# A hybrid attention and RG-LRU layer: the end of each recurrent block moved into the next block's projection

## The chip, the cores and the metric

The kernel runs on one core of one Trainium2 chip. The metric is the device time of one execution in microseconds (us). A TensorE clock of 1.00 in the profile is 2.4 GHz, 0.50 is 1.2 GHz.

## The reference, cut to what matters

One layer of a decoder on 16 meta tokens and 1024 tokens of width 2048. The normalised input goes through one projection to q, k, v, g_a, u and g_r; eight heads of differential attention and eight recurrent blocks of 128 channels are gated, put side by side and multiplied with `w_out`. The recurrent part is the one that the change touches:

```python
u = conv4(u) + conv_b                                  # causal, per channel
ub = u.reshape(B, T, N_LRU_BLOCKS, LRU_BLOCK)
r = sigmoid(einsum('btnc,ncd->btnd', ub, w_a) + b_a)   # two gates, a 128 x 128
i = sigmoid(einsum('btnc,ncd->btnd', ub, w_x) + b_x)   # matrix per block each
log_a = -LRU_C * r * softplus(-lru_lambda)
a = exp(log_a)
b = sqrt(-expm1(2.0 * log_a)) * i * u                  # factor 1 at position 0
h = scan(h = a * h + b)                                # over the positions
rec = h * silu(g_lru)
```

## The kernel before

Channels lie on the partitions, positions along the free dimension. The work is done in two halves: half A has the 16 meta tokens and 512 positions, half B the other 512. The order in time is: attention heads of A, recurrent blocks of A (some 463 to 642 us), attention heads of B, recurrent blocks of B (some 1111 to 1308 us, at first between the parts of the last head), then the output projection. Every matmul in fp32 is made of three in fp32r: the operands are split in a high and a low part (`split`, line 77: the high part by ScalarE, the low one by VectorE), and high x high, high x low and low x high are summed in PSUM.

`proj` (line 135) is one projection of 128 channels: 16 steps `kt` of three matmuls (L158 to L160), into one PSUM bank per job. `load_w` loads the weights in two parts of eight `kt` each: a raw tile by SyncE's queue (two buffers), then `whi` and `wlo` by `split` (three buffers each). A job names its bank by a tag: "proj" (two banks), "S" (three), "T" (two) or "pv" (one). `midway` is a function that `proj` calls after half of the steps; what it issues, and the matmuls behind it are tied to come after the instruction that it returns. Before the change only the first head used it.

A recurrent block is made by `lru` (line 523) of two projections, u and g. In half A u has two jobs, of 272 and 256 columns, one after the other; in half B it has one of 512. g has 512 columns in both. When the last job of u is done, its sink calls `finish` (line 464): the convolution in four steps on VectorE (L467, then L470 three times), the split into `uh` and `ul`, for each of the two gates three matmuls into banks "S" or "T" (L485 to L487; in half A twice, by columns) and a sigmoid (L488), and the recurrence up to the scan (L492 to L502). The sink of g (`g_sink`, line 509) takes `gx` from the bank (L512), and makes the sigmoid, the products and the DMA of the result (`emit_mix`, L430, on POOL's queue) that later work loads. The convolution's input `ue`, `uc`, `sg` and `gx` have one buffer each.

In half A two loads of half B's input (`step`, lines 175 to 191, scaled on ScalarE and VectorE in L187 to L190) and one for its squares (`squares`, L200) are issued on POOL's queue after each u projection, and tied to come after the last `emit_mix`. In half B loads of earlier results for the output projection (`load_mix`, L619) are issued after u and g of blocks 1 to 4, behind the last weight load on SyncE's queue.

Tiles and waits are set by a framework that also orders each engine's instructions at build time, by simulated times and buffers (`schedule_with_timeline_sim`, line 939); `issue_after` adds only an order on one engine's queue. So the order of the code isn't the order in the trace. In the last attention head of half B, `pv` collects the products with v (L405 to L407), `att` is read from it (L413), and `ms` takes the same single bank for the norm (L418, L419; read last by L424).

Of the kernel before, what the change touches and what calls it, by code (L numbers as in the profile page):

```python
# [66 lines left out]
class Trunk:  # L67
# [67 lines left out]
    def proj(self, *groups, midway=None):  # L135


        nc = self.nc
        work = []
        for m, jobs in groups:  # L140
            ws = self.load_in(m, 0, 2) if isinstance(m, int) else m
            if len(groups) == 1:
                work += [[(ws, j)] for j in jobs]
            else:
                work.append([(ws, j) for j in jobs])
        if len(groups) > 1:
            work = [sum(work, [])]
        for unit in work:
            acc = [self.ps.tile([P, 512], F32, tag=j[3], name="proj", bufs={"S": 3, "pv": 1}.get(j[3], 2)) for _, j in unit]
            with ExitStack() as order:  # L150
                for kt in range(KT):
                    if kt == 8 and midway:
                        order.enter_context(self.tc.issue_after(midway().ins))
                    c = slice((kt % 8) * P, (kt % 8) * P + P)
                    for (ws, (hT, c0, n, _, _)), ps in zip(unit, acc):
                        hi, lo = ws[kt // 8]
                        xh, xl = hT[0][kt][:, c0:c0 + n], hT[1][kt][:, c0:c0 + n]
                        nc.tensor.matmul(ps[:, :n], lhsT=hi[:, c], rhs=xh, start=(kt == 0), stop=False)  # L158
                        nc.tensor.matmul(ps[:, :n], lhsT=hi[:, c], rhs=xl, start=False, stop=False)  # L159
                        nc.tensor.matmul(ps[:, :n], lhsT=lo[:, c], rhs=xh, start=False, stop=(kt == KT - 1))  # L160
            for (_, j), ps in zip(unit, acc):
                j[4](ps)
# [279 lines left out]
    def lru_part(self, b, half, pool, tl, gw, carry):  # L442
# [7 lines left out]
        def u_sink(c0, w):  # L450
            def f(ps):
                if c0 == 0:
                    state["ue"] = ue = pool.tile([P, 3 + LA], F32, tag="ue", name="ue", bufs=1)
                    if half:
                        nc.vector.tensor_copy(out=ue[:, 0:3], in_=carry[:, 0:3])
                    else:
                        nc.vector.memset(ue[:, 0:3], 0.0)
                nc.vector.tensor_tensor(out=state["ue"][:, 3 + c0:3 + c0 + w], in0=ps[:, :w],
                                        in1=self.rstd[:, half * LA + c0:half * LA + c0 + w], op=ALU.mult)
                if c0 + w == n:  # L460
                    state["h"] = finish()
            return f

        def finish():
            ue = state["ue"]
            uc = pool.tile([P, LA], F32, tag="uc", name="uc", bufs=1)[:, :n]
            nc.vector.tensor_scalar(out=uc, in0=ue[:, 3:3 + n], scalar1=par[:, 3:4], scalar2=par[:, 4:5],  # L467
                                    op0=ALU.mult, op1=ALU.add)
            for i in range(3):
                nc.vector.scalar_tensor_tensor(out=uc, in0=ue[:, i:i + n], scalar=par[:, i:i + 1], in1=uc,  # L470
                                               op0=ALU.mult, op1=ALU.add)
            uh = tl.tile([P, n], F32R, tag="pth", name="uh", bufs=1 + half)
            ul = tl.tile([P, n], F32R, tag="ptl", name="ul", bufs=1 + half)
            self.split(uh, ul, uc)
            if not half:
                nc.vector.tensor_copy(out=carry[:, 0:3], in_=ue[:, n:n + 3])
            gates = []
            for g in range(2):
                o = tl.tile([P, n], F32, tag=("eg", "gr")[g], name="gate", bufs=gb)
                for c0, w in ([(0, 512)] if half else [(0, 272), (272, 256)]):  # L480
                    x = "T" if g and not half else "S"
                    ps = self.ps.tile([P, 512], F32, tag=x, name=x, bufs={"S": 3, "T": 2}[x])
                    c = slice(c0, c0 + w)
                    wh, wl = gw[0][:, g * P:(g + 1) * P], gw[1][:, g * P:(g + 1) * P]
                    nc.tensor.matmul(ps[:, :w], lhsT=wh, rhs=uh[:, c], start=True, stop=False)  # L485
                    nc.tensor.matmul(ps[:, :w], lhsT=wh, rhs=ul[:, c], start=False, stop=False)
                    nc.tensor.matmul(ps[:, :w], lhsT=wl, rhs=uh[:, c], start=False, stop=True)  # L487
                    nc.scalar.activation(o[:, c], ps[:, :w], AF.Sigmoid, bias=par[:, 5 + g:6 + g])  # L488
                gates.append(o)
            r, gi = gates  # L490
            th = tl.tile([P, n], F32, tag="tmp", name="th", bufs=gb)
            nc.scalar.activation(th, r, AF.Tanh, scale=self.negc[:, b:b + 1])  # L492
            nc.scalar.activation(r, r, AF.Exp, scale=self.posc[:, b:b + 1])
            d = pool.tile([P, LA], F32, tag="dd", name="dd", bufs=1 + half)[:, :n]
            nc.scalar.activation(d, r, AF.Square)
            nc.vector.scalar_tensor_tensor(out=th, in0=d, scalar=1.0, in1=th, op0=ALU.add, op1=ALU.mult)
            self.last_sqrt = nc.scalar.activation(th, th, AF.Sqrt)
            if not half:
                nc.vector.memset(th[:, 0:1], 1.0)
            nc.vector.tensor_tensor(out=gi, in0=gi, in1=uc, op=ALU.mult)  # L500
            nc.vector.tensor_tensor(out=gi, in0=gi, in1=th, op=ALU.mult)
            nc.vector.tensor_tensor_scan(out=d, data0=r, data1=gi,  # L502
                                         initial=carry[:, 3:4] if half else 0.0,
                                         op0=ALU.mult, op1=ALU.add)
            if not half:
                nc.vector.tensor_copy(out=carry[:, 3:4], in_=d[:, n - 1:n])
            return d

        def g_sink(ps):
            sg = pool.tile([P, HALF], F32, tag="sg", name="sg", bufs=1)  # L510
            gx = pool.tile([P, HALF], F32, tag="gx", name="gx", bufs=1)
            nc.vector.tensor_tensor(out=gx, in0=ps, in1=self.rstd[:, META + half * HALF:META + (half + 1) * HALF],  # L512
                                    op=ALU.mult)
            self.last_sigmoid = nc.scalar.activation(sg, gx, AF.Sigmoid)
            nc.vector.tensor_tensor(out=sg, in0=gx, in1=sg, op=ALU.mult)
            hst = state["h"]
            o = 0 if half else META
            nc.vector.tensor_tensor(out=sg, in0=sg, in1=hst[:, o:o + HALF], op=ALU.mult)
            self.emit_mix(half, H + b, sg)

        return u_sink, g_sink

    def lru(self, b, half, pool, tl, hT, tag="proj", g_tag="proj"):
        gw = self.lru_weights(b, pool)
        if not half:
            if b == 0:
                self.carry_all = self.const.tile([P, 32], F32, name="carry")
            self.carry[b] = self.carry_all[:, 4 * b:4 * b + 4]
        us, gs = self.lru_part(b, half, pool, tl, gw, self.carry[b])
        chunks = [(0, HALF)] if half else [(0, 272), (272, 256)]  # L530
        return ((M_U + b, [(hT, c0, w, tag, us(c0, w)) for c0, w in chunks]),
                (M_GR + b, [(hT, 0 if half else META, HALF, g_tag, gs)]))


    def setup0(self):
# [245 lines left out]
    def build(self):  # L781
# [67 lines left out]
        with ExitStack() as s:  # L849
            pool = s.enter_context(tc.tile_pool(name="lruA", bufs=1, side="left", reuse_waits="tile"))  # L850
            pb = s.enter_context(tc.tile_pool(name="prepB", bufs=1, side="left", reuse_waits="tile"))
            self.sq_bufs = 1
            step, squares, fin_b = self.prep(pb, nc.gpsimd, self.xb, HALF, 1, hTB, LA, 2)
            for b in range(8):
                for m, jobs in self.lru(b, 0, pool, pool, hTA):
                    self.proj((m, jobs))
                    if m < M_GR:
                        with tc.issue_after(self.last_mix.ins):
                            for i in range(2 * b, 2 * b + 2):
                                step(i)  # L860
                            squares(b)
            fin_b()
        left.close()

# [9 lines left out]
        m1 = fin.enter_context(tc.tile_pool(name="m1", bufs=1, side="left", reuse_waits="tile"))  # L874
        mixA = []
        with tc.tile_pool(name="lruB", bufs=1, side="left", reuse_waits="tile") as pool:
            for b in range(8):
                for m, jobs in self.lru(b, 1, pool, tl, hTB, *("T" if b == 1 else "proj",) * 2):
                    self.proj((m, jobs))
                    if 1 <= b < 5:  # L880
                        with tc.issue_after(self.last_w.ins):
                            for _ in range(2):
                                mixA.append(self.load_mix(m1, 0, len(mixA)))
        tail.close()
        right.close()
        ps_cm.__exit__(None, None, None)
# [56 lines left out]
```

## Time and profile before

| | us |
|---|---|
| median of three runs | 1642.99 |
| lowest and highest | 1640.56 and 1643.88 |
| the profiled execution | 1637.0 |
| its span, first to last instruction | 1635.2 |
| TensorE busy | 1596.9 |
| VectorE busy | 1117.6 |
| ScalarE busy | 874.1 |

Times in the rows are in us from the first instruction of the profiled execution. PE is TensorE, DVE VectorE, ACT ScalarE, POOL GpSimd, PEld TensorE's loading of weights. "[2.16 <-ACT uh L79]" at the end of a row means that the engine stood idle for 2.16 us before it, until ScalarE had written `uh` in line 79.

### The profile page before, as it was taken

What the parts mean: (1) busy time and instruction counts of PE and PEld (TensorE: products, weight loads), DVE (VectorE), ACT (ScalarE), POOL (GpSimd) and SP (SyncE); (2) the same over time, 40 slices, a digit from 0 to 9 for tenths busy, and PEclk for the clock granted to TensorE, in tenths of its full rate; (3) what the DMA queues carried; (4) which work ended last, traced back from release to release, by engine and by line L of the source; (5) the groups of instructions that cost most, each with busy time, mean ns of one, the idle gap of its engine ahead of it and who ended that gap; (6) DMA issues with size and microseconds to landing.
All of it is one profiled execution on the core that took longest, in us unless ns stands there. A gap on an engine that the chain in (4) does not pass through costs nothing.

```text
span 1635.2 us, 22985 instructions
## 1 busy us (share of the span) xinstructions
PE 1596.9 (98%) x8466; PEld 1370.8 (84%) x8466; DVE 1117.6 (68%) x2218; ACT 874.1 (53%) x1392; POOL 205.2 (13%) x308
## 2 busy tenths in 40 slices
PE   7999999999999999999999999999999999899996
PEld 6889889998989888888888888887887887788885
DVE  6766556665676667667668667757877656867996
ACT  5655555545566657456556556545776543332533
POOL 1211111110011010201011001000000002200262
PEclk9999999999999999999999999999999999999999
DMA  9633344333344443533234234233443388969874
GB/s 310 206 121 109 116 137 132 122 124 108 122 146 145 145 142 123 183 114 116 84 120 134 78 120 123 78 97 100 138 138 114 120 309 290 326 234 330 307 283 154
DMA packets 85196, 261.61 MB, mean 160 GB/s; under 512 B 11659, under 2 KB 13748, under 8 KB 84956
## 3 DMA queue, kind: packets, MB, share of 16 engines
q1 hardware_dynamic: 60544, 192.18, 35.2%
q0 software_dynamic: 24304, 67.90, 12.6%
q8 instruction: 67, 1.10, 0.3%
q14 instruction: 45, 0.37, 0.1%
q10 hardware_dynamic: 236, 0.06, 0.0%
HBM read 213.35 MB, written 39.86 MB: 155 GB/s over the span
## 4 chain that ended last, share of the span: by engine, by line
PE 75%; DVE 8%; issue 7%; DMA 7%; ACT 3%; POOL 1%; SPq 0%; ACTq 0%; DVEq 0%; POOLq 0%
PE proj L158 20%; PE proj L159 19%; PE proj L160 19%; PE T L396 2%; PE o L685 2%; PE o L686 2%; PE o L684 2%; DVE wlo L80 2%; PE S L341 2%; PE S L339 2%; DMA wb<-w_out 1%; DVE y L700 1%; DVE wb L658 1%; DMA xb<-mix_d 1%; DMA xt<-x 1%
## 5 line engine op out<-in xcount | busy, mean ns | idle before, releaser
L158 PE MATMUL proj<-hTA,whi 128*128 128x256 f32 (+2 forms) x1152 | 373.5, 325 | 1.9 <-ACT whi L79 1.9
L159 PE MATMUL proj<-hTA,whi 128*128 128x256 f32 (+2 forms) x1152 | 370.4, 322 | 0.0
L160 PE MATMUL proj<-hTA,wlo 128*128 128x256 f32 (+2 forms) x1152 | 369.5, 322 | 0.5 <-DVE wlo L80 0.5
L79 ACT ACTIVATE whi<-wraw 128x1024 fp32r<-128x1024 f32 (+1 forms) x218 | 228.2, 1047 | 244.8 <-PE proj L159 186.6
L80 DVE TENSOR_TENSOR wlo<-wraw,whi 128x1024 fp32r<-128x1024 f32 (+1 forms) x218 | 264.0, 1212 | 116.5 <-ACT whi L79 116.3
L158 PE MATMUL proj<-hTB,whi 128*128 128x512 f32 x768 | 302.1, 393 | 1.2 <-DVE gr L291 0.6
L160 PE MATMUL proj<-hTB,wlo 128*128 128x512 f32 x768 | 300.9, 392 | 0.0
L159 PE MATMUL proj<-hTB,whi 128*128 128x512 f32 x768 | 299.8, 390 | 0.0
L158 PEld LDWEIGHTS proj<-hTA,whi 128*128 128x128 f32 x1152 | 218.8, 190 | 18.7 <-ACT whi L79 2.6
L160 PEld LDWEIGHTS proj<-hTA,wlo 128*128 128x128 f32 x1152 | 218.7, 190 | 16.3 <-DVE wlo L80 0.7
L159 PEld LDWEIGHTS proj<-hTA,whi 128*128 128x128 f32 x1152 | 219.0, 190 | 14.4
L685 PE MATMUL o<-wlo,mix 128*128 128x512 f32 x416 | 163.2, 392 | 7.9 <-DVE wlo L80 7.9
L158 PEld LDWEIGHTS proj<-hTB,whi 128*128 128x128 f32 x768 | 144.3, 188 | 30.4 <-DVE gr L291 2.6
L160 PEld LDWEIGHTS proj<-hTB,wlo 128*128 128x128 f32 x768 | 144.2, 188 | 30.1
L159 PEld LDWEIGHTS proj<-hTB,whi 128*128 128x128 f32 x768 | 144.3, 188 | 28.6
L686 PE MATMUL o<-whi,mix 128*128 128x512 f32 x416 | 162.6, 391 | 0.0
L684 PE MATMUL o<-whi,mix 128*128 128x512 f32 x416 | 162.5, 391 | 0.0
L358 ACT ACTIVATE s<-s,st 128x144 f32<-128x144 f32 (+7 forms) x128 | 100.0, 782 | 50.9 <-DVE st L356 50.1
L685 PEld LDWEIGHTS o<-wlo,mix 128*128 128x128 f32 x416 | 78.4, 189 | 26.4 <-DVE wlo L80 10.0
L351 DVE TENSOR_SCALAR_CACHE_REDUCE s<-S,b 128x256 f32<-128x256 f32 (+5 forms) x176 | 82.6, 477 | 19.4 <-PE S L341 16.2
L684 PEld LDWEIGHTS o<-whi,mix 128*128 128x128 f32 x416 | 78.5, 189 | 16.6 <-ACT gate L488 0.3
L686 PEld LDWEIGHTS o<-whi,mix 128*128 128x128 f32 x416 | 78.5, 189 | 16.2
(240 smaller groups left out, 2357.6 us busy)
## 6 DMA issues: line engine op xcount, KB each, us to landing
wraw<-w_in SPq DMA_DIRECT2D x190, 512.0 KB, 4.0
wraw<-w_out SPq DMA_DIRECT2D x48, 512.0 KB, 4.3
mix<-mix_d SPq DMA_DIRECT2D x48, 256.0 KB, 5.1
wb<-w_out SPq DMA_DIRECT2D x24, 512.0 KB, 5.1
t_d<-wb POOLq DMA_DIRECT2D x16, 512.0 KB, 6.8
xb<-mix_d SPq DMA_DIRECT2D x24, 256.0 KB, 6.4
kk_d<-kk POOLq DMA_DIRECT2D x8, 528.0 KB, 3.0
kk<-kk_d POOLq DMA_DIRECT2D x8, 528.0 KB, 4.1
```

The costliest lines, as they stand in the source:

```text
L79: nc.scalar.activation(hi, src, AF.Copy)
L80: nc.vector.tensor_tensor(out=lo, in0=src, in1=hi.bitcast(F32), op=ALU.subtract)
L158: nc.tensor.matmul(ps[:, :n], lhsT=hi[:, c], rhs=xh, start=(kt == 0), stop=False)
L159: nc.tensor.matmul(ps[:, :n], lhsT=hi[:, c], rhs=xl, start=False, stop=False)
L160: nc.tensor.matmul(ps[:, :n], lhsT=lo[:, c], rhs=xh, start=False, stop=(kt == KT - 1))
L339: nc.tensor.matmul(ps[:, :w], lhsT=qq[:, j, qc], rhs=kk[:, j, c0:c0 + w], start=True, stop=False)
L341: nc.tensor.matmul(ps[:, :w], lhsT=self.qz[:, j, qc], rhs=kl[:, c0:c0 + w], start=False, stop=True)
L351: nc.vector.tensor_scalar(out=s[j][:, a:a + n], in0=ps[:, a - c0:a - c0 + n], scalar1=self.b31[:, h:h + 1], scalar2=-3.0e38, op0=ALU.add, ...
L358: nc.scalar.activation(s[j][:, :s_len], s[j][:, :s_len], AF.Exp, bias=nm[:, j:j + 1], accum_out=l[:, j:j + 1])
L684: nc.tensor.matmul(acc, lhsT=x[:, 0, tk], rhs=w[0], start=start, stop=False)
L685: nc.tensor.matmul(acc, lhsT=x[:, 0, tk], rhs=w[1], start=False, stop=False)
L686: nc.tensor.matmul(acc, lhsT=x[:, 1, tk], rhs=w[0], start=False, stop=stop)
```

## The change

`finish` is cut in three. `convolve` holds the convolution and the split; the sink of u still calls it. `recur` holds the gates, the recurrence and the scan. The new `finish` calls `recur`, then does what the sink of g did; that sink only keeps the bank now. `finish` is handed to the next block's `proj` of u as `midway`, which calls it after `kt` 7 of the first job; in that job the matmuls of `kt` 8 to 15 are tied behind the last gate matmul. After block 7 `finish` is called by itself. g of block 0 keeps a "proj" bank, g of all other blocks goes to the single bank "pv"; in half B u of block 1 keeps "T".

```diff
         for unit in work:
+            hook, midway = midway, None
             acc = [self.ps.tile([P, 512], F32, tag=j[3], name="proj", ...) for _, j in unit]
             with ExitStack() as order:
                 for kt in range(KT):
-                    if kt == 8 and midway:
-                        order.enter_context(self.tc.issue_after(midway().ins))
+                    if kt == 8 and hook:
+                        order.enter_context(self.tc.issue_after(hook().ins))
...
                 if c0 + w == n:
-                    state["h"] = finish()
+                    convolve()
...
-        def finish():
+        def convolve():
...
+            state["u"] = uc, uh, ul
+
+        def recur():
+            uc, uh, ul = state["u"]
             gates = []
...
-                    nc.tensor.matmul(ps[:, :w], lhsT=wl, rhs=uh[:, c], start=False, stop=True)
+                    last = nc.tensor.matmul(ps[:, :w], lhsT=wl, rhs=uh[:, c], start=False, stop=True)
...
-            return d
+            state["h"] = d
+            return last
 
         def g_sink(ps):
+            state["g"] = ps
+
+        def finish():
+            last = recur()
+            ps = state["g"]
             sg = pool.tile([P, HALF], F32, tag="sg", name="sg", bufs=1)
...
             self.emit_mix(half, H + b, sg)
+            return last
...
-                (M_GR + b, [(hT, 0 if half else META, HALF, g_tag, gs)]))
+                (M_GR + b, [(hT, 0 if half else META, HALF, "pv" if b else "proj", gs)]), finish)
...
+            finish = None
             for b in range(8):
-                for m, jobs in self.lru(b, 0, pool, pool, hTA):
-                    self.proj((m, jobs))
+                u, g, then = self.lru(b, 0, pool, pool, hTA)
+                for m, jobs in (u, g):
+                    self.proj((m, jobs), midway=finish if m < M_GR else None)
...
+                finish = then
+            finish()
             fin_b()
...
-                for m, jobs in self.lru(b, 1, pool, tl, hTB, *("T" if b == 1 else "proj",) * 2):
-                    self.proj((m, jobs))
+                u, g, then = self.lru(b, 1, pool, tl, hTB, "T" if b == 1 else "proj")
+                for m, jobs in (u, g):
+                    self.proj((m, jobs), midway=finish if m < M_GR else None)
...
+                finish = then
+            finish()
```

## Rows read from the trace of the kernel before

**Rows 1.** The page, part 1: busy us, share of the span, instructions.
```profile
PE 1596.9 (98%) x8466; PEld 1370.8 (84%) x8466; DVE 1117.6 (68%) x2218; ACT 874.1 (53%) x1392; POOL 205.2 (13%) x308
```

**Rows 2.** Who waits for whom, TensorE, whole span: us in total, times, longest.
```profile
PE S L485 <- ACT uh L79: 3.9, 4, 2.2
...
PE S L486 <- DVE ul L80: 0.7, 3, 0.2
```

**Rows 3.** One block of half A: us; busy PE, PEld, DVE, ACT, POOL; clock, DMA, GB/s.
```profile
560.80:589.10 28.30, 25.92 (x157) 23.61 (x156) 18.49 (x31) 17.02 (x24) 2.67 (x5) 0.94 0.38 126
```

**Rows 4.** Timeline of TensorE in that block: start, us, engine, line, operation.
```profile
563.84 0.51 PE L485 MATMUL S<-uh,lwh 128*128 128x272 f32 x2 [2.16 <-ACT uh L79]
...
565.18 0.59 PE L486 MATMUL S<-ul,lwh 128*128 128x272 f32 x1 [0.22 <-DVE ul L80]
```

**Rows 5.** Busy us by stretch, after that wait and around one of half B.
```profile
564.00:567.00 3.00, 2.78 (x15) 2.56 (x16) 3.00 (x5) 2.97 (x5) 0.00 (x0) 0.64 0.43 139
567.00:570.00 3.00, 3.00 (x22) 3.00 (x22) 1.54 (x3) 2.98 (x7) 0.54 (x1) 0.79 0.51 195
1236.00:1239.00 3.00, 1.95 (x9) 1.29 (x8) 2.93 (x6) 1.01 (x2) 0.00 (x0) 1.00 0.53 168
```

**Rows 6.** Timeline of POOL in half A, before that wait.
```profile
550.06 0.55 POOL L430 DMA_DIRECT2D mix_d<-sg  x1 [7.62 <-DVE sg L518]
553.43 1.07 POOL L179 DMA_DIRECT2D xraw<-xb  x2 [2.82 <-issue]
```

**Rows 7.** Timeline of TensorE, the waits of half B.
```profile
1213.38 0.74 PE L485 MATMUL S<-uh,lwh 128*128 128x512 f32 x2 [0.43 <-ACT uh L79]
...
1237.83 0.74 PE L485 MATMUL S<-uh,lwh 128*128 128x512 f32 x2 [1.05 <-ACT uh L79]
```

**Rows 8.** Timeline of TensorE, half A: a u projection's first matmul, the gates.
```profile
536.59 0.29 PE L158 MATMUL proj<-hTA,whi 128*128 128x272 f32 x1
...
537.33 0.40 PE L485 MATMUL S<-uh,lwh 128*128 128x272 f32 x2
```

**Rows 9.** Timeline of TensorE, half B: matmuls 1 and 25 of u, block 1; the gates.
```profile
1141.65 0.39 PE L158 MATMUL proj<-hTB,whi 128*128 128x512 f32 x1
...
1147.48 0.39 PE L158 MATMUL proj<-hTB,whi 128*128 128x512 f32 x1
...
1164.74 0.62 PE L485 MATMUL S<-uh,lwh 128*128 128x512 f32 x2
```

**Rows 10.** Timeline of VectorE at the start of half B's recurrence.
```profile
1147.11 0.69 DVE L414 TENSOR_TENSOR sq<-att 128x512 f32<-128x512 f32 x1 [3.94 <-ACT att L413]
...
1148.38 0.54 DVE L467 TENSOR_SCALAR uc<-ue,lru_par_sb 128x512 f32<-128x512 f32 x1
...
1155.77 1.22 DVE L80 TENSOR_TENSOR wlo<-wraw,whi 128x1024 fp32r<-128x1024 f32 x1
1156.91 1.29 DVE L80 TENSOR_TENSOR mix<-mix 128x512 fp32r<-128x512 f32 x2
1158.11 0.74 DVE L470 SCALAR_TENSOR_TENSOR uc<-ue,lru_par_sb,uc 128x512 f32<-128x512 f32 x1
...
1161.51 0.68 DVE L80 TENSOR_TENSOR ul<-uc,uh 128x512 fp32r<-128x512 f32 x1
1164.96 0.69 DVE L424 TENSOR_TENSOR eg<-ms,eg 128x512 f32<-128x512 f32 x1 [2.77 <-ACT ms L423]
```

**Rows 11.** Timeline of ScalarE in the same stretch.
```profile
1159.79 0.61 ACT L79 ACTIVATE uh<-uc 128x512 fp32r<-128x512 f32 x1
```

**Rows 12.** Timeline of TensorE, end of half B: a gate's last matmul, the output projection.
```profile
1307.16 0.39 PE L487 MATMUL S<-uh,lwl 128*128 128x512 f32 x1
...
1308.33 0.50 PE L684 MATMUL o<-whi,mix 128*128 128x512 f32 x1
```

**Rows 13.** Timeline of VectorE in half A: g read from its bank, the scan.
```profile
489.86 0.68 DVE L512 TENSOR_TENSOR gx<-proj,rstd 128x512 f32<-128x512 f32 x1
...
499.49 1.26 DVE L502 TENSOR_TENSOR_SCAN dd<-gate 128x528 f32<-128x528 f32 x1
```

More of the change, by code (lines that the diff above doesn't have):

```diff
@@ L519, in g_sink, with lru @@
             self.emit_mix(half, H + b, sg)
-        return u_sink, g_sink
-    def lru(self, b, half, pool, tl, hT, tag="proj", g_tag="proj"):
+            return last
+        return u_sink, g_sink, finish
+    def lru(self, b, half, pool, tl, hT, tag="proj"):
         gw = self.lru_weights(b, pool)
@@ L528, in lru @@
             self.carry[b] = self.carry_all[:, 4 * b:4 * b + 4]
-        us, gs = self.lru_part(b, half, pool, tl, gw, self.carry[b])
+        us, gs, finish = self.lru_part(b, half, pool, tl, gw, self.carry[b])
         chunks = [(0, HALF)] if half else [(0, 272), (272, 256)]
         return ((M_U + b, [(hT, c0, w, tag, us(c0, w)) for c0, w in chunks]),
-                (M_GR + b, [(hT, 0 if half else META, HALF, g_tag, gs)]))
+                (M_GR + b, [(hT, 0 if half else META, HALF, "pv" if b else "proj", gs)]), finish)
     def setup0(self):
@@ L876, in build @@
         with tc.tile_pool(name="lruB", bufs=1, side="left", reuse_waits="tile") as pool:
+            finish = None
             for b in range(8):
-                for m, jobs in self.lru(b, 1, pool, tl, hTB, *("T" if b == 1 else "proj",) * 2):
-                    self.proj((m, jobs))
+                u, g, then = self.lru(b, 1, pool, tl, hTB, "T" if b == 1 else "proj")
+                for m, jobs in (u, g):
+                    self.proj((m, jobs), midway=finish if m < M_GR else None)
                     if 1 <= b < 5:
```

## The prediction

> **What bounds the kernel now.** I read the page first: TensorE is busy 1596.9 of 1635.2 us [rows 1], so the end moves only when TensorE waits less or more than now. The second view is who waits for whom on TensorE: on the gate matmuls (L485 to L487) it waits 3.9 + 0.7 us in seven places [rows 2]. That is nearly all it loses in the two recurrent stages, and all that this change can aim at. A split by block finds the costliest place, a block of half A with 25.92 us busy of 28.3 and the clock at 0.94 [rows 3]. The timeline of that block shows why: 2.16 us until the split `uh` of the convolved input is there, 0.22 more for `ul` [rows 4]. Behind the waiting matmul stood matmuls of the u projection that needed nothing: TensorE takes its queue in order. After this wait the granted clock is 0.64 and 0.79 in two stretches of 3 us, so 1.08 + 0.63 = 1.7 us more are lost; after a wait of 1.05 us it stays at 1.00 [rows 5].
>
> Two things then decide: where in the queue the gates stand, and when `uh` comes. The order on each engine is made at build time from simulated times, and it isn't the traced one. In half A the gates of a block already run six matmuls into the next block's u projection (536.59 to 537.33 at 0.123 us each) [rows 8]. So in half A the change makes a move of 18 matmuls, not of a stage. In half B the gates stand elsewhere in each block, and at its start lies the row that matters most: the first matmul of u of block 1 runs at 1141.65, but the gates of block 0 only at 1164.74 [rows 9], 98 matmuls later (48 of u, 48 of g, two of block 2; with five others between them, 0.22 to 0.23 us each). TensorE runs a block ahead of VectorE there, because VectorE and ScalarE still end the last attention head.
>
> **Part 1: the waits in the recurrent stages.** Half B has 0.43 + 1.05 us [rows 7]. After the change these gates stand behind 24 matmuls of the next u projection, some 5 us later (24 at 0.23 us), so these waits go: **-1.5**. Half A has the rest of 3.9 + 0.7 us [rows 2], 3.1 us, and the 1.7 us of clock. Its gates move by 18 x 0.123 = 2.2 us, as much as the longest wait. Against that: `uh` was late because the convolution's steps stand on VectorE and ScalarE behind the scaling of `xb`, whose load is queued on POOL behind the mix of the block before (550.06, the load at 553.43) [rows 6]. That mix comes from the gates, so it moves by 2.2 us too. If the order stays, nothing is gained; if the load, now later, lets the convolution go ahead of it, 3.1 + 1.7 = 4.8 go. Of the long wait 2.82 us was POOL's own, for nothing that the profile shows [rows 6], and without that it would have cost no clock; so I take the clock and half of the waits, **-3.3** (ends 0 and -4.8). A hidden cost here: with the load later, the split of the next weights stands behind it on ScalarE; that is in the end at 0.
>
> **Part 2: the gates of block 0 in half B.** The change puts kt 8 to 15 of u of block 1 behind the gates of block 0 in TensorE's queue. In the kernel before these 24 matmuls, the 48 of g of block 1 and two more ran in front of them. From 1147.48, when the 24th matmul has been issued [rows 9], TensorE may only run what stands elsewhere. g of block 1 now goes to the bank `pv`, which the last head's `ms` holds until L424 at 1164.96 [rows 10]. The weights of block 2's u need one of the three `whi` buffers: two are held by g of block 1 and one by the half of u that is held up. What is left is L418 and L419, two matmuls, 0.45 us.
>
> So TensorE waits until `uh` and `ul` are there. The convolution's first step runs at 1148.38, its last at 1158.11, `uh` at 1159.79 to 1160.40 [rows 10, 11]. Its four steps take 0.54 + 3 x 0.74 = 2.8 us, but between them VectorE's queue holds other work that was ready: ends of the head, splits of weights and of mix. Most of that stays, for it doesn't hang on TensorE. One split of weights, `wlo` at 1155.77, goes: it needs a buffer that the held half keeps. It took 1.14 us up to the next start, 1156.91 [rows 10]. The last step ends then at 1158.85 - 1.14 = 1157.7, `uh` is done 0.65 later at 1158.4, `ul` 0.7 later (0.68 in [rows 10]). TensorE waits 1158.4 - 1147.5 - 0.45 = 10.5 us and 0.2 for `ul`: **+10.7**. Ends: the four steps without anything between them give 1148.38 + 2.8 + 0.65 = 1151.8, a wait of 4.3 us; with the times as they were, `ul` ends at 1162.19 and the wait is 1162.2 - 1147.5 - 0.9 = 13.8. I take 10.7, nearest to the order that the rows have. Any of these is longer than the 2.16 us that cost clock, so **+1.7**; a wait in two pieces could cost it twice (end 3.4). In later blocks nothing comes of it: VectorE's delay behind TensorE is used up once.
>
> **Part 3: the ends of the stages.** The last gates of half B ran ahead of the last matmuls of g; now they stand behind all of g, and the output projection behind them. Its first matmul ran 1.17 us after the L487 that ends the first gate [rows 12], as soon as ScalarE had read the bank. With the second gate's two matmuls alone in between (three slots of 0.23, 0.7 us), 0.5 us is left: **+0.5** (ends 0, and 1.8 if a table load of 1.28 us falls there). In half A the last gates already run inside the attention's q projection, so their place stays; the last `xb` loads and `fin_b` come up to 2.2 us later, with q's 48 matmuls, 11 us, ahead of their first use: 0 (end 2). The mix DMAs of each block, on POOL ahead of the `xb` loads, are counted in part 1; in half B no load stands behind them. `gx`, the sigmoid of g and the products move with `finish` and have a block of time: VectorE is busy 18.49 of 28.3 us in the block of [rows 3].
>
> **The sum.** On the profiled execution of 1637.0 us (span 1635.2 and 1.8 around it): -1.5 - 3.3 + 10.7 + 1.7 + 0.5 = +8.1, so 1645.1. That execution was 6.0 us under the median of the runs, 1642.99; I put the change on the median: **1651.1 us**. By the ends: -1.5 - 4.8 + 4.3 + 1.7 + 0 = -0.3, and -1.5 + 0 + 13.8 + 3.4 + 3.8 = +19.5.
>
> **Rivals.** First, on the other side: the convolution of block 0 gets ahead of the end of the head, and TensorE never waits. VectorE stands idle for 3.94 us before 1147.11 [rows 10], with the input `ue` there; four steps of 2.8 us and `uh` of 0.65 would end at 1143.2 + 3.45 = 1146.6, before 1147.5, the point from which it decides. Then -1.5 - 3.3 + 0.5 = -4.3: 1638.7. Against it: that gap lay open in the kernel before too, and L467 runs only after L414 and L415, which wait for `att`, the head's last PV product [rows 10]. Chance 0.14.
>
> Second, a short wait: VectorE's steps follow each other, the low end above: 4.3 + 1.7 - 4.3 = +1.7, so 1644.7, which can't be told from no change. For it: a starved TensorE leaves less other work. Chance 0.16.
>
> Third: one bank for the gate. If VectorE reads g only after the scan, as `finish` is written, the next g waits for its bank. From the gates to the mix is 550.06 - 537.33 = 12.7 us [rows 6, 8]; in half B the rest of u and the gates cover 30 x 0.23 = 6.9 of it, in half A 84 x 0.123 = 10.3, so six blocks each wait 5.8 and 2.4 us: +49 on the forecast, some 1700 us. Against it: before the change `gx` is traced behind the recurrence as well, and ran at 489.86, ahead of the scan at 499.49 [rows 13]. The Trainium skill (Perfetto Trace Analysis, Optimizing Tensor Performance, Matmuls) speaks for this rival: independent groups of matmuls should rotate through different PSUM banks, so that reading one out overlaps the matmuls of the next, which one bank can't. By that rule it would be likely; the early `gx` is why I don't follow it. Chance 0.04.
>
> That the change does little of what it says holds for half A, where the gates were in the next u projection already; that is the end at 0.
>
> **Chances.** The forecast has 0.64, of which 0.06 fall within the bound below; 0.02 is left for what I haven't seen. A difference of 0.2%, 3.3 us, is about what a measurement of this kernel can tell from no change. Faster 0.14 + 0.01 = 0.15, within it 0.16 + 0.06 = 0.22, slower 0.58 + 0.04 + 0.01 = 0.63. The range reaches from just below the first rival's time, 1638.5, to 1660, short of the high end of the sum, since not all high ends come at once; it leaves out the third rival and the outermost ends, some 0.15.
>
> **What would show it.** Right: one wait of TensorE of 4 to 14 us, in one or two pieces, at the start of half B's recurrence, on L485 for `uh`, with the clock down behind it, and no waits over 0.3 us on the gates afterwards in half B. Gates 24 matmuls into each u projection. Part 1 is wrong in half A if waits on L485 or on new weights remain. The forecast is wrong if `uh` of block 0 comes before TensorE's 24th matmul, or if something else fills the gap; the third rival would show as waits on L158 for `gx`.

## The result

The changed kernel takes 1648.97 us (median of five, 1648.29 to 1651.25) where the kernel before, run beside it, takes 1640.56 (median of five, 1638.15 to 1643.88): a ratio of **1.0056, 95% interval 1.0041 to 1.0072**, slower by some 9 us. A second set of runs gave 1.0049 (1.003 to 1.0067). The forecast was 1651.1, slower. The profiled execution of the changed kernel took 1648.45 us, its span is 1646.7.

Lines have moved: the gates are L490 to L492 (L485 to L487 in the rows before), their sigmoid L493, the last head's `ms` L419 and L420, Ln and Exp L422 and L423, the last reader of `ms` L425, the convolution L468 and L471.

The page, part 1, and who waits for whom on TensorE (us in total, times, longest), to be read against [rows 1, 2]:

```profile
PE 1598.9 (97%) x8466; PEld 1371.6 (83%) x8466; DVE 1118.5 (68%) x2218; ACT 874.4 (53%) x1392; POOL 204.9 (12%) x308
```

```profile
PE S L490 <- ACT uh L79: 8.2, 1, 8.2
...
PE ms L419 <- ACT pth L79: 6.9, 2, 3.9
...
PE ms L420 <- DVE ptl L80: 1.1, 1, 1.1
```

No engine does more work. The seven waits on the gates [rows 2] have become one of 8.2 us; two shorter ones on `ms` stand before it (of the 6.9 us on L419, 3.0 are in an earlier stage). Two stages moved in opposite directions. Busy time by stretch (us; busy PE, PEld, DVE, ACT, POOL; clock, DMA, GB/s). The first stretch is the recurrence of half A, from 10 us behind its first u matmul to the first matmul of half B's q projection. The second is the recurrence of half B, from the first u matmul of block 1 to the first output matmul. Before:

```profile
447.10:638.30 191.20, 188.06 (x1186) 171.24 (x1185) 126.56 (x203) 115.93 (x159) 19.98 (x37) 0.99 0.43 141
...
1141.70:1308.30 166.60, 165.05 (x726) 135.40 (x725) 116.94 (x164) 109.59 (x140) 8.13 (x15) 1.00 0.39 126
```

After:

```profile
446.00:632.20 186.20, 186.20 (x1199) 170.95 (x1198) 129.97 (x209) 117.32 (x161) 20.00 (x37) 1.00 0.44 146
...
1133.70:1314.30 180.60, 167.42 (x728) 137.15 (x727) 117.42 (x166) 109.45 (x139) 8.11 (x15) 0.96 0.35 114
```

Half A is shorter by 5.0 us, though it now holds the 12 gate matmuls of block 7 that ran behind its end before: TensorE is busy all the time. Half B is longer by 14.0: TensorE stands for 13.2 us in place of 1.6, and is 2.4 us longer busy with the same work.

**Half A.** One block, the one that answers to [rows 3, 4]: the window, then VectorE, ScalarE and the gate on TensorE.

```profile
557.40:581.60 24.20, 24.20 (x158) 22.27 (x158) 17.19 (x28) 17.32 (x24) 2.66 (x5) 1.00 0.44 144
```

```profile
551.39 2.37 DVE L471 SCALAR_TENSOR_TENSOR uc<-ue,lru_par_sb,uc 128x528 f32<-128x528 f32 x3
558.04 0.49 DVE L188 TENSOR_SCALAR hTB<-xraw,g_col 128x512 fp32r<-128x512 f32 x1 [4.27 <-DMA xraw<-xb]
```

```profile
558.03 0.63 ACT L79 ACTIVATE uh<-uc 128x528 fp32r<-128x528 f32 x1
```

```profile
561.53 0.29 PE L490 MATMUL S<-uh,lwh 128*128 128x272 f32 x1
```

The three later steps of the convolution run in one go, ahead of the scaling that waits for `xraw`; `uh` ends at 558.66, 2.9 us before the gate. Over the eight blocks this lead is 1.9 to 7.3 us; before it was 0.05 us in three blocks.

**The start of half B's recurrence.** TensorE, then VectorE, then ScalarE, to be read against [rows 9 to 11]:

```profile
1133.67 0.39 PE L159 MATMUL proj<-hTB,whi 128*128 128x512 f32 x1
...
1143.56 0.50 PE L419 MATMUL ms<-pth,ones 128*128 128x512 f32 x1 [3.89 <-ACT pth L79]
1145.11 0.79 PE L420 MATMUL ms<-ptl,ones 128*128 128x512 f32 x1 [1.05 <-DVE ptl L80]
1154.14 1.22 PE L490 MATMUL S<-uh,lwh 128*128 128x512 f32 x2 [8.24 <-ACT uh L79]
```

```profile
1140.40 0.54 DVE L468 TENSOR_SCALAR uc<-ue,lru_par_sb 128x512 f32<-128x512 f32 x1
...
1147.78 0.68 DVE L421 SCALAR_TENSOR_TENSOR eg<-ms,eg 128x512 f32<-128x512 f32 x1
...
1149.58 0.74 DVE L471 SCALAR_TENSOR_TENSOR uc<-ue,lru_par_sb,uc 128x512 f32<-128x512 f32 x1
...
1153.57 0.69 DVE L425 TENSOR_TENSOR eg<-ms,eg 128x512 f32<-128x512 f32 x1 [2.84 <-ACT ms L424]
```

```profile
1149.05 1.28 ACT L422 ACT_TABLE_LOAD   x1
1150.34 0.63 ACT L422 ACTIVATE sq<-eg 128x512 f32<-128x512 f32 x1
1150.98 1.28 ACT L423 ACT_TABLE_LOAD   x1
1152.28 0.63 ACT L423 ACTIVATE sq<-sq 128x512 f32<-128x512 f32 x1
1152.94 0.60 ACT L424 ACTIVATE ms<-sq 128x512 f32<-128x512 f32 x1
1153.48 0.61 ACT L79 ACTIVATE uh<-uc 128x512 fp32r<-128x512 f32 x1
```

Between the 24th matmul of u, which ends at 1139.67, and the first gate TensorE runs two matmuls and stands for 3.89 + 1.05 + 8.24 = 13.2 us. The convolution is over at 1150.32, but ScalarE had begun the last head's Ln 1.3 us earlier, with two table loads, Exp and a square in the queue ahead of `uh`: 3.2 us from the last step to the start of `uh`. What let Ln begin so early is L421 on VectorE, which reads `ms` and is now ahead of the convolution's last step. In the kernel before (L420 there) it stood behind that step, which began at 1158.11 [rows 10]:

```profile
1159.11 0.68 DVE L420 SCALAR_TENSOR_TENSOR eg<-ms,eg 128x512 f32<-128x512 f32 x1
```

The clock, in the stretch of the wait and in the two behind it:

```profile
1139.70:1154.10 14.40, 1.29 (x2) 0.47 (x2) 11.13 (x20) 12.28 (x18) 1.08 (x2) 0.67 0.28 91
1154.10:1160.70 6.60, 6.56 (x20) 5.25 (x21) 2.06 (x4) 1.28 (x1) 0.54 (x1) 0.68 0.10 40
1160.70:1163.70 3.00, 3.00 (x14) 2.46 (x14) 1.11 (x2) 2.27 (x5) 0.54 (x1) 1.00 0.00 0
```

It falls to its lower level during the wait: in stretches of 3 us it is 0.94 from 1142 to 1145, 0.50 from there to 1157 and 0.79 from 1157 to 1160, so from about 1144.6 to 1158.3. The first matmuls after the wait run slowly. From there on no gate of half B waits; `uh` ends 0.7 to 7.7 us ahead of them.

### The profile page after: what moved, and what is told of

It reads as the page before. It is cut to its first block, busy times and chain, and to the rows that moved or that the text cites. A ratio compares the mean times of both kernels' runs of the same rounds, so it can differ in the third digit from the quotient of the medians.

```text
span 1646.7 us, 22971 instructions
## 1 busy us (share of the span) xinstructions
PE 1598.9 (97%) x8466; PEld 1371.6 (83%) x8466; DVE 1118.5 (68%) x2218; ACT 874.4 (53%) x1392; POOL 204.9 (12%) x308
## 5 line engine op out<-in xcount | busy, mean ns | idle before, releaser
L160 PEld LDWEIGHTS proj<-hTA,whi 128*128 128x128 f32 x1152 | 218.9, 190 | 14.4
L698 PE MATMUL o<-wlo,mix 128*128 128x512 f32 x416 | 164.3, 395 | 10.7 <-DVE wlo L80 10.6
L352 DVE TENSOR_SCALAR_CACHE_REDUCE s<-S,b 128x256 f32<-128x256 f32 (+5 forms) x176 | 82.7, 477 | 14.4 <-PE S L342 12.3
```

What stands on the lines that cost most here:

```text
L352: nc.vector.tensor_scalar(out=s[j][:, a:a + n], in0=ps[:, a - c0:a - c0 + n], scalar1=self.b31[:, h:h + 1], scalar2=-3.0e38, op0=ALU.add, ...
L698: nc.tensor.matmul(acc, lhsT=x[:, 0, tk], rhs=w[1], start=False, stop=False)
```

## The experiments

The stages of all profiled executions, cut at the same rows: "A" runs from 10 us behind half A's first u matmul to the first matmul of u of block 1 in half B (the recurrence of half A and the heads of half B; the matmuls of block 7's gates, which change sides, are inside), "B" from there to the first output matmul, "out" from there to the last matmul. "Idle" is the time in B in which TensorE stood.

| kernel | ratio (95%) | A | B | idle | out |
|---|---|---|---|---|---|
| before | 1 | 694.6 | 166.6 | 1.6 | 318.1 |
| before_again | | 695.6 | 165.9 | 1.1 | 318.0 |
| after | 1.0056 (1.0041–1.0072) | 687.7 | 180.6 | 13.2 | 323.6 |
| after_again | 1.0049 (1.003–1.0067) | 687.7 | 182.2 | 13.8 | 320.2 |
| a_only | 0.9952 (0.9935–0.997) | 688.0 | 165.6 | 1.0 | 321.4 |
| b_only | 1.0088 (1.0066–1.011) | 694.5 | 182.8 | 15.4 | 320.4 |
| hook_kt2 | 0.9999 (0.9984–1.0013) | 697.4 | 166.5 | 1.5 | 318.7 |
| uh_vector | 1.008 (1.0061–1.0099) | 692.9 | 180.9 | 12.0 | 322.8 |
| pinned_T | 1.0055 (1.0035–1.0075) | 687.9 | 180.0 | 11.1 | 320.9 |
| unpinned_pv | 0.9993 (0.9982–1.0004) | 687.6 | 169.7 | 4.2 | 320.5 |
| unpinned_T | 1.0007 (0.9993–1.0021) | 687.5 | 175.8 | 6.8 | 321.7 |
| pins_proj | 1.0006 (0.9994–1.0018) | 687.6 | 175.2 | 5.9 | 320.9 |
| unpinned_all | 0.9956 (0.9939–0.9973) | 688.5 | 164.0 | 0.0 | 320.5 |

**One half at a time.** In each of these two, one half calls the gates and the rest where the kernel before did. a_only puts this into the changed kernel, with g of half B back in its old banks and the hook out of half B's loop; b_only does the same with half A.

```diff
                 if c0 + w == n:
                     convolve()
+                    if half == 1:
+                        recur()
...
         def g_sink(ps):
             state["g"] = ps
+            if half == 1:
+                finish()
...
-            last = recur()
+            last = recur() if half != 1 else None
```

> The change in half A alone; half B as in the kernel before. If the changed kernel's two stages are independent, this one gets half A's gain (no waits of TensorE on the gates of half A, 3.1 us, and no fall of the clock behind them, 1.7 us) and none of half B's loss: 4.8 us less than before, about 1635.8, ratio 0.997, no wait over 2 us at the start of half B. If the late output projection of the changed kernel (5.5 us longer in its trace) comes with half A's reordering, the ratio is 1.000.

Measured 0.9952: 7.9 us less than before (4.9 to 10.7), with no wait of TensorE on any gate of half A, and half B as it was. The gain is larger than the 4.8 us expected; stage A alone has 6.6.

> The change in half B alone; half A as in the kernel before. If half B's start carries the loss, TensorE waits some 13 us between the 24th matmul of u of block 1 and the gates of block 0, with the clock down behind it, and half B costs 12 to 14 us: 1653 to 1655, ratio 1.008. If the 5.5 us of the output projection come with half B's change, 1658, ratio 1.011. If half B cost only what the changed kernel lost as a whole, ratio 1.0056.

Measured 1.0088: 14.4 us more (10.8 to 18.0). The waits at half B's start are there with the same sizes (3.9, 1.0 and 8.2 us). Another wait of 2.1 us, which the changed kernel doesn't have, stands at the end of the stage: the first output matmul waits for the sigmoid of a gate, which runs on ScalarE behind a table load of 1.28 us at 1320.90.

```profile
1323.46 0.50 PE L701 MATMUL o<-whi,mix 128*128 128x512 f32 x1 [2.08 <-ACT gate L495]
```

So the change is a gain of about 8 and a loss of about 14 us. Their sum, 6.5 us (1.9 to 11.1), agrees within the noise with the 9.2 and 8.0 us of the two sets of runs of the changed kernel; nothing shows that the two halves touch each other, but a few us couldn't be seen.

**The same program again**, both kernels, for what differs between two executions.

> The changed kernel once more, as a control for what differs between two profiled executions of one program. If the output projection's 5.5 us are chance of one execution, this trace has it 1 to 6 us shorter, with one fall of the clock in it, or with other places; if they belong to the program (three steps on VectorE and ScalarE stand in another order there), it has the same waits at the same places, 12.4 us in all. The ratio is 1.0056 in either case.

> The kernel before once more, as a control: how far the stages of two profiled executions of one program lie apart. If the output projection's length is chance, it lies between 318 and 324 us here as in the other runs, with another number of waits than the 9.7 us of the first execution; if 318.1 us belongs to the program, it comes out within 0.5 us of it.

The output stage took 323.6 and 320.2 us in two executions of the changed kernel, 318.1 and 318.0 in two of the one before. So some 3 us of the 5.5 were that execution's own. That the other 2 belong to the change doesn't follow: a_only has 321.4, and hook_kt2, a variation of it, 318.7. One thing that differs is how often the clock falls before the stage's last matmul: once and not at all in the two executions of before, once in hook_kt2 and in pinned_T, two or three times in the others. It isn't the whole of it, for pinned_T takes 320.9 us. What decides the length stays open.

**Where half A's gain comes from.** a_only with the gates after 6 matmuls of the next u projection, where they ran before [rows 8].

```diff
-    def proj(self, *groups, midway=None):
+    def proj(self, *groups, midway=None, at=8):
...
-                    if kt == 8 and hook:
+                    if kt == at and hook:
...
-                    self.proj((m, jobs), midway=finish if m < M_GR else None)
+                    self.proj((m, jobs), midway=finish if m < M_GR else None, at=2)
```

> The change in half A alone, with the gates issued after 6 matmuls of the next u projection (at kt 2) in place of 24, where they ran before the change. If half A's gain comes from the later place of the gates, which lets the convolution go ahead of the scaling of xb, the waits of about 3 us on the gates come back, half A's recurrence takes 190 to 191 us and the ratio is 0.999 to 1.000. If it comes from issuing the recurrence apart from the convolution, half A's recurrence stays at 186.1 us and the ratio at 0.995.

The gain is gone (0.9999), and the waits are back: 5.8 us in eight places, `A` 9 us longer than in a_only. VectorE's timeline shows why, in the block that answers to the one above:

```profile
556.87 0.77 DVE L473 SCALAR_TENSOR_TENSOR uc<-ue,lru_par_sb,uc 128x528 f32<-128x528 f32 x1
563.87 0.75 DVE L191 SCALAR_TENSOR_TENSOR hTB<-xraw,g_col,hTB 128x512 fp32r<-128x512 f32 x1 [6.23 <-ACT hTB L190]
564.54 0.76 DVE L473 SCALAR_TENSOR_TENSOR uc<-ue,lru_par_sb,uc 128x528 f32<-128x528 f32 x1
```

With the gates early the scaling of `xb` stands between the second and the third step again, and VectorE stands idle for 6.23 us before it. So not the issue of the recurrence apart from the convolution makes the gain, but its place: only with the later gates does the convolution get ahead. This execution also says what waits cost beside their length. At full clock throughout, its recurrence of half A has 186.85 us of busy TensorE (x1186):

```profile
448.80:641.50 192.70, 186.85 (x1186) 169.92 (x1185) 125.68 (x202) 115.94 (x159) 19.92 (x37) 1.00 0.42 140
```

The 186.20 (x1199) of the changed kernel are 184.8 without the 12 gate matmuls of block 7 (0.12 us each), and here there are eight waits, there none.

**What ScalarE's queue costs at half B's start.** The changed kernel, with `uh` of block 0 of half B written by VectorE.

```diff
-            self.split(uh, ul, uc)
+            if half and b == 0:
+                nc.vector.tensor_scalar(out=uh, in0=uc, scalar1=1.0, scalar2=None, op0=ALU.mult)
+                nc.vector.tensor_tensor(out=ul, in0=uc, in1=uh.bitcast(F32), op=ALU.subtract)
+            else:
+                self.split(uh, ul, uc)
```

> As the changed kernel, but uh of block 0 in half B is written by VectorE in place of ScalarE, which had two table loads, Ln, Exp and Square of the last head in its queue ahead of it. If those make up the part of the wait that the prediction had not counted, uh comes 3 us earlier, the wait before the first gate matmul falls from 8.2 to about 5.2 us, and half B's recurrence to 177.5. If the wait is set by VectorE, it gets 0.6 us longer.

TensorE's timeline there (L494 is the gate; the copy of L456, named as what ended its wait, follows the write of `uh` on VectorE):

```profile
1150.85 0.79 PE L419 MATMUL ms<-pth,ones 128*128 128x512 f32 x1 [3.89 <-ACT pth L79]
1152.40 0.80 PE L420 MATMUL ms<-ptl,ones 128*128 128x512 f32 x1 [0.76 <-DVE ptl L80]
1158.43 1.19 PE L494 MATMUL S<-uh,lwh 128*128 128x512 f32 x2 [5.24 <-DVE ue L456]
1161.59 0.80 PE L159 MATMUL proj<-hTB,whi 128*128 128x512 f32 x1 [1.97 <-DVE eg L425]
```

The wait before the gate fell from 8.24 to 5.24 us, as expected if ScalarE's Ln and Exp hold `uh` back. But 1.97 us came back at once: the next matmuls, of g of block 1, wait until L425 has read `ms` out of `pv`, which comes at 1161.54 in that run. So stage B didn't come down to 177.5. (Its stage A is 5 us longer; 3.2 of that is a wait for the load of `qq` in the heads, which the two executions of the changed kernel don't have.)

**The bank and the pin.** pinned_T keeps the order of the changed kernel and gives g of block 1 the bank T. unpinned_pv keeps the banks and leaves kt 8 to 15 of u of block 1 free to run before the gates of block 0. unpinned_T does both.

```diff
-                (M_GR + b, [(hT, ..., HALF, "pv" if b else "proj", gs)]), finish)
+                (M_GR + b, [(hT, ..., HALF, "T" if half and b == 1 else "pv" if b else "proj", gs)]), finish)
```

```diff
-                        order.enter_context(self.tc.issue_after(hook().ins))
+                        last = hook()
+                        if last is not None:
+                            order.enter_context(self.tc.issue_after(last.ins))
...
+                if b == 1:
+                    first = finish
+                    finish = lambda: first() and None
```

> As the changed kernel, with g of block 1 in bank T in place of pv in half B, so that it can run while kt 8 to 15 of u of block 1 are held. Its 48 matmuls are 10.9 us of work. If the bank decides, the wait at half B's start falls from 13.2 to 2 or 3 us, the clock doesn't fall, and half B's recurrence comes to 168 to 170 us, ratio 0.997. If the lag has to be paid once anyway, it stays near 176 us, with the waits further back, ratio 1.000. If something else than the bank holds g back, 180.6 us and ratio 1.005 as in the changed kernel.

> As the changed kernel, but kt 8 to 15 of u of block 1 need not stand behind the gates of block 0; g of block 1 stays in pv. If the pin alone makes the wait, the 24 held matmuls fill 5.5 us of it and at most 7.7 of the 13.2 us are left at the start, held by pv. If what is lost is a lag of VectorE and ScalarE behind TensorE that must be paid once, wherever it shows, half B's recurrence (first u matmul of block 1 to the first output matmul) stays near the 175.8 us of the run with bank T, in waits further back, and the ratio is 1.000 to 1.003. If the lag were not what counts, it is 167 to 170 us and the ratio 0.997.

> As the changed kernel, but in half B the matmuls kt 8 to 15 of u of block 1 need not stand behind the gates of block 0, and g of block 1 keeps its bank T as in the kernel before. If the pin and the bank together make the wait at half B's start, that wait of 13.2 us is gone, the gains stay, and the time is 6.3 us under the kernel before (4.8 of half A, 1.5 of half B): 1634.3, ratio 0.996. If VectorE's and ScalarE's late start in half B costs TensorE its wait wherever the gates stand, the wait comes back one block later and the ratio is near 1.005.

All three lose the long wait at the start, and none keeps half A's gain as a_only does. In unpinned_pv four short waits of 4 us in all are left in the first 35 us of the stage, 2.7 of them on weights and 1.3 on `uh`. In the other two TensorE waits further back, for `uh` and for weights that VectorE or ScalarE split late. Who waits for whom on TensorE in that stage, for pinned_T:

```profile
PE S L490 <- ACT uh L79: 5.0, 4, 2.3
PE proj L161 <- DVE wlo L80: 3.6, 4, 2.0
PE proj L159 <- ACT whi L79: 2.6, 1, 2.6
```

and for unpinned_T:

```profile
PE proj L163 <- DVE wlo L80: 3.2, 2, 2.2
PE S L492 <- ACT uh L79: 2.5, 1, 2.5
PE proj L161 <- DVE gx L525: 1.1, 2, 0.6
```

With the pin taken from block 1 alone (unpinned_pv) the stage is 10.9 us shorter than in the changed kernel. With the bank opened alone (pinned_T) it is 0.6 shorter, though the long wait is gone there too: the closed bank decides where TensorE stands, not how much the stage loses. A lag of fixed size that has to be paid once doesn't fit: the idle time is 4.2, 6.8 or 11.1 us. The order pinned for blocks 1 to 7 and the single bank `pv` were left as suspects.

**Which of the two.** pins_proj (the first diff) is unpinned_T with g of half B in its old banks; unpinned_all (the second, in half B's loop) is unpinned_T with no block of half B pinned.

```diff
-                (M_GR + b, [(hT, ..., HALF, "T" if half and b == 1 else "pv" if b else "proj", gs)]), finish)
+                (M_GR + b, [(hT, ..., HALF, ("T" if b == 1 else "proj") if half else "pv" if b else "proj", gs)]), finish)
```

```diff
-                finish = then
+                finish = lambda f=then: f() and None
```

> As the run with block 0 unpinned and bank T, with the pins of blocks 1 to 7, but g of blocks 2 to 7 of half B in the two proj banks as in the kernel before. If the one gate bank pv makes the waits in the later blocks, they go: 166 to 168 us for half B's recurrence, ratio 0.995 to 0.996. If the pins make them, 174 to 176 us and ratio 1.000.

> As the run with block 0 unpinned and bank T, but no block of half B is pinned: gates, recurrence and end of a block are issued at kt 8 of the next u projection, and TensorE's matmuls need not stand behind them. If the 6.8 us of waits in the later blocks of that run come from the pins of blocks 1 to 7, they go, half B's recurrence takes 165 to 167 us as in the run with half A alone, and the ratio is 0.995 to 0.996. If they come from the late issue of the recurrence's steps on VectorE and ScalarE, or from the one gate bank pv, they stay, 174 to 176 us, ratio 1.000.

Two banks in place of one make no difference that can be told: 175.2 against 175.8 us, with ratios of 1.0006 and 1.0007, where two executions of the changed kernel lie 1.6 us apart in this stage. The 1.1 us of waits for `gx`, which the single bank makes in unpinned_T, are gone, but 2.9 us of waits for `ue` have come. Without pins stage B takes 164.0 us, TensorE doesn't stand in it at all, and the ratio is 0.9956. So in half B the pin is the cause, in the later blocks too. How it works is seen at block 2: the gates of block 1 on TensorE and `ue` of block 2 on VectorE, first in unpinned_T, then in unpinned_all.

```profile
1175.58 0.62 PE L492 MATMUL S<-uh,lwh 128*128 128x512 f32 x2
```

```profile
1185.70 0.68 DVE L461 TENSOR_TENSOR ue<-proj,rstd 128x512 f32<-128x512 f32 x1
```

```profile
1173.10 0.62 PE L492 MATMUL S<-uh,lwh 128*128 128x512 f32 x2
```

```profile
1171.83 0.66 DVE L461 TENSOR_TENSOR ue<-proj,rstd 128x512 f32<-128x512 f32 x1
```

With the pin, u of block 2 can only be complete after the gates of block 1, and its `ue` comes 10.1 us behind them; without, it comes 1.3 us ahead of them. The pin closes a loop: gates, second half of the next u, `ue`, convolution, `uh`, the next gates. From gates to gates it took 25.2 and 24.6 us there, where the 102 matmuls of a block, 0.227 us apart, are 23.2 us. In the changed kernel itself the loop keeps to 23.1 us after the first blocks and costs nothing more. In unpinned_pv too `ue` of block 2 comes 11.6 us behind the gates of block 1 (1181.84 and 1170.22), and from gates to gates it takes 23.7 us there and 23.1 from then on. Why the loop is long in one build and short in another is not settled; VectorE's order differs between them.

a_only and unpinned_all both beat the kernel before, by 0.48% and 0.44%; their intervals overlap almost wholly.

## Why the prediction was right, and where by luck

The time (1651.1, measured 1648.97), the sign and the mechanism came out; two terms were off, in opposite directions.

**What bounds the kernel:** right. The differences in the two recurrent stages are waits of TensorE, its clock, and some 2 us of longer busy time that come with the waits.

**Part 1, half A: -3.3, measured about -7 in the trace (694.6 to 687.7) and -7.9 by a_only.** This is beyond the end of -4.8. The step that decides was seen, "if the load, now later, lets the convolution go ahead of it", but its waits were counted by half, in case the order stays. hook_kt2 shows it turn with the gates' place. All 3.1 us of waits and the 1.7 of clock went. POOL's own 2.82 us, from which the working argued for the half, came again in that block and cost TensorE nothing:

```profile
551.88 1.07 POOL L180 DMA_DIRECT2D xraw<-xb  x2 [2.83 <-issue]
```

The rest of some 2 us was no term of the sum: TensorE's busy time for the same work is longer in an execution with waits, 2 us over eight waits in hook_kt2 at full clock. Half B's 1.5 us of waits on gates went as well, as forecast.

**Part 2, the start of half B: +10.7 and +1.7 of clock, measured 13.2 and about 2.4** (busy TensorE 167.42 against 165.05). The place, the held 24 matmuls, the missing split `wlo` and the closed bank `pv` are as forecast. Mis-sized is the step "`uh` is done 0.65 later". The last step of the convolution ended 16.65 us after u's first matmul, where the working has 16.05; but `uh` was done at 20.4 in place of 16.75. The `ms` matmuls ran directly behind the 24th of u, so L421, which reads `ms`, ran on VectorE at 1147.78, ahead of the convolution's last step (before it ran at 1159.11, behind it), and so Ln and Exp got ahead of `uh` on ScalarE. uh_vector took those 3 us off the wait. I had moved the convolution on VectorE and not asked what else moves ahead of `uh` on ScalarE. Also, L419 and L420 didn't fill the gap early: they waited for the head's own chain, 3.9 us. The wait came in three pieces with one fall of the clock.

**"In later blocks nothing comes of it":** right for the changed kernel, by the slack of 0.7 us and more, but not as a rule. With the long wait at the start removed, 4.2 (unpinned_pv, in the first 35 us), 6.8 and 11.1 us (unpinned_T and pinned_T, further back) were still lost in kernels that kept the pins of the later blocks; without any pin nothing was.

**Part 3: +0.5, measured 0.** The last gate matmul starts at 1314.03 and the first output matmul at 1314.25, the distance of a matmul that doesn't wait. The working's upper end, a table load ahead of the gate's sigmoid, did come in b_only, with 2.1 us. The output stage, 5.5 us longer in the profiled execution and 2.1 in the next, was no step of mine; its cause is open.

**The rivals.** The convolution of block 0 didn't get ahead of the head's end: its first step runs behind L415 and L416, as in [rows 10]. The same mechanism did decide half A. The short wait (4.3 us) fell with the order on VectorE, which kept most of its other work between the steps. The single gate bank cost nothing in the changed kernel, where no matmul waits for `gx`. The rule of the Trainium skill (Perfetto Trace Analysis, Optimizing Tensor Performance, Matmuls) that independent groups should rotate through different banks doesn't decide here: pins_proj has 1.0006 and unpinned_T 1.0007. The closed `pv` at the start, held by another user, set the place of the long wait, and only behind the pin.

By the timed runs of one half each the sum is -7.9 + 14.4 = +6.5, where +8.1 was forecast: -3.3 for half A and +11.4 for half B (-1.5 + 10.7 + 1.7 + 0.5). The result came out close by luck, because half A's gain and half B's loss were both too small in the sum, by 4.6 and 3.0. The medians differ by 8.4 us, 0.3 from the forecast difference; the 2.1 us between 1651.1 and 1648.97 come from the kernel before, whose median was 1642.99 when the forecast was made and 1640.56 beside the changed kernel.

## What to carry to other kernels

Where work is moved to a fixed place in an in-order queue, ask what the place holds back: 24 matmuls tied behind a late operand cost more than the waits that the move removed, and the tie made a loop through three engines that can cost again in later blocks. Half B without the tie lost nothing, and half A, where the tie stayed, kept its gain. And when a chain of steps on one engine is moved, look at the queue of every engine that the chain passes: here two table loads on ScalarE, off the path before, came onto it.

## What the runs showed of the hardware

Ln and Exp of the last head each have a table load of 1.28 us in front, with Exp directly behind Ln (1149.05 and 1150.98 above). The Trainium skill (ScalarE: Activation LUTs, Table sets: the hidden batching unit) counts ln and then exp as one load, since one set has both. In this case's trace there are two for this head, and the second was 1.28 us of TensorE's longest wait. But they are the only ones on these two lines, with 16 heads in all. The instructions of L422, durations in ns (least, median, most), first and last start in us:

```profile
L422 ACT ACTIVATE sq<-eg x16: 629/632/635, 114.2 to 1150.3; 128x512 f32<-128x512 f32 x16
...
L422 ACT ACT_TABLE_LOAD  x1: 1283/1283/1283, 1149.0 to 1149.0; - x1
```

The kernel asks for the common set by name ahead of each half's heads (L551 and L886, `preload_act_table_set`), and the 15 other heads run Ln and Exp without a load. Only the last head comes behind another load, that of a sigmoid at 1140.54. Whether asking for the set once more there would save a load was not run.

A wait of 3.9 us, a short one and one of 8.2 brought the clock to its lower level in the middle, at 1144.6, and it stayed there for 4.2 us after the gate matmuls had begun (1154.14 to 1158.3). In hook_kt2 waits of 1.60 and 1.12 us, with 0.6 us of matmuls between them, in a block like that of [rows 4], left the clock at 1.00, where one of 2.16 had cost 1.7 us [rows 5].

```profile
567.10 0.51 PE L492 MATMUL S<-uh,lwh 128*128 128x272 f32 x2 [1.60 <-ACT uh L79]
...
568.85 0.39 PE L493 MATMUL S<-ul,lwh 128*128 128x272 f32 x1 [1.12 <-DVE ul L80]
```
